# Mixer attention with the values stationary, the next layer's modulation gated by x, and the context's feed-forward moved ahead in the side work

## The chip, the cores and the metric

The kernel runs on one core of a Trainium2 chip. The time is that of one execution in device microseconds (us); a kernel's figure is the median of several runs. One run was taken with the hardware profiler, and all rows below come from that one.

## The reference, cut to what matters

A first block (gated spatial mixing, differential attention, a mixture of experts) is followed by a second block of two layers on two streams of 256 tokens by 1024 channels, `x` and `ctx`. The change touches the second block alone:

```
for layer in range(2):
    mx = split(silu(c) @ ada_w[layer] + ada_b[layer], 9)      # shifts, scales, gates of x
    mc = split(silu(c_ctx) @ ada_w[layer] + ada_b[layer], 9)  # the same of ctx
    x   = x   + 0.5*mx[2]*swiglu(modulate(rms_norm(x),   mx[0], mx[1]), gu1, down1)
    ctx = ctx + 0.5*mc[2]*swiglu(modulate(rms_norm(ctx), mc[0], mc[1]), gu1, down1)
    q, k, v, pool, fft of both streams = modulated norms @ w_in
    s = q @ k_all.T * scale;  p = softmax(s);  ax = p @ v_all   # 8 heads, 2 key/value heads
    x = x + mx[5] * concat(ax, pool mixer, fourier mixer) @ w_out
    x = x + 0.5*mx[8]*swiglu(modulate(rms_norm(x), mx[6], mx[7]), gu2, down2)
    if layer == 0: the same attention (over ctx alone), mixer and second swiglu for ctx
```

## The kernel before, in words

Everything is float32. A weight tile of 128x1024 is loaded by SP's queue into `raw`, split by ACT into `whi` (line 93) and by DVE into `wlo` (line 94), and used in three matmuls (lines 127 to 129: high by high, low by high, high by low). Activations are split alike: `hT` holds a stream's normalised channels, `T[:, 0]` those of x and `T[:, 1]` those of ctx. A helper, `norm_hT`, makes them: squares on ACT, a chain of some ten narrow DVE instructions for the inverse root (lines 146 to 157), the scaled rows `xs` (line 171, DVE), transposes on PE (line 133), then ACT and DVE write `hT`.

A feed-forward (`ffn`) is cut into 11 blocks of 256 hidden channels. A block needs four weight tiles for the gate and up halves and two for the down half. Where both streams work on a block together the matmuls are 512 columns wide and the weights are loaded once; where a stream is alone, the gate and up matmuls are 256 wide and the weights are loaded for it by itself. `CA` gives the blocks of the second feed-forward of layer 0 that ctx does alone beside x's attention (`side`), `EC` the cuts of the shared pass.

The modulation of layer 1 (`ada`, `L = 1`) is a generator of 72 steps. Each loads 128x1024 of `ada_w` into a tile `araw` and multiplies it on DVE with two vectors, summing into a column (lines 853 and 854: two instructions a step). It is advanced as weight tiles are asked for (`rate`), but its steps depend on nothing in the layer, so a gate holds them back: at step 0 the columns are first written by a copy from the tile `self.gate`, and no step can run before that copy's source has been written.

In the mixer, an attention unit is one (row half `tt`, head pair `hp`, key/value head `kv`): two score matmuls (line 1120), a maximum on DVE (1122), the exponential with its sum `s` on ACT (1124), transposes of `e` on PE (133, four for x, two for ctx), a copy to `aT` by ACT or DVE, and the product with `v` (line 1134) into the PSUM tile `po`, of which there is one. An attention of x has 16 units of 512 keys, that of ctx 16 of 256. `run(main, *rest, n)` interleaves one step of `main` with `n` of the rest. The pool mixer loads a 128x512 matrix `poolc` four times per stream into one buffer; the Fourier mixer is a short chain of matmuls.

A scheduler that estimates times writes the final order of every engine's instructions; each engine then executes its own list strictly in order.

Of the kernel before, what the change touches and what calls it, by code (L numbers as in the profile page):

```python
# [6 lines left out]
F32 = mybir.dt.float32  # L7
# [3 lines left out]
AF = mybir.ActivationFunctionType  # L11
OP = mybir.AluOpType
# [30 lines left out]
TG = ("tr",)*4  # L43
AH = 1
ME = 3
MA = 2
MP = 2
MC = 1
W1 = (4,4,4)
CA = (0, 3)  # L50
EC = (3, 6, 9, 11)
FC = (2, 6, 9, 11)
class Builder:
    def __init__(self, tc, A):
# [859 lines left out]
    def ffn(self, P, L, f, parts, cuts, pre="", ends=()):  # L914

        nc = self.nc
        gu, dn = f"gu{f}", f"dn{f}"  # L920
        nb = 7 if pre else 2 * max(b - a for a, b in zip(cuts, cuts[1:])) + 2
        for streams, c0, c1 in zip(parts, cuts, cuts[1:]):
            n = 256 * len(streams)
            act = streams[0][2] if len(streams) == 1 else self.both
            hid = []
            for j in range(c0, c1):
                if pre:
                    pp = [self.mm([128, 2, 256]) for c in range(2)]
                    pgu = [[pp[c][:, w] for c in range(2)] for w in range(2)]
                else:  # L930
                    pgu = [[self.mm([128, n], tag) for c in range(2)] for tag in ("mm", "at")]
                for w in range(2):
                    for b in range(2):
                        wt = self.W(gu, (L, 22 * w + 2 * j + b))
                        for c in range(2):
                            p = pgu[w][c] if n == 256 else pgu[w][c].rearrange("p (a b) -> p a b", a=2)
                            self.proj_T(p, [wt, wt], c, act, range(4 * b, 4 * b + 4))
                for c in range(2):
                    s = self.t(P, [128, n], F32, pre + "silu", 2)
                    fh = self.t(P, [128, n], F32R, pre + "fh", nb)  # L940
                    fl = self.t(P, [128, n], F32R, pre + "fl", nb)
                    if self.tanh:

                        nc.scalar.activation(out=s, in_=pgu[0][c], func=AF.Tanh, scale=0.5)
                        nc.vector.scalar_tensor_tensor(out=s, in0=s, scalar=1.0, in1=pgu[0][c], op0=OP.add, op1=OP.mult)
                        nc.vector.tensor_tensor(out=s, in0=s, in1=pgu[1][c], op=OP.mult)
                        nc.scalar.activation(out=fh, in_=s, func=AF.Copy, scale=0.5)
                        nc.vector.scalar_tensor_tensor(out=fl, in0=s, scalar=0.5, in1=fh.bitcast(F32), op0=OP.mult, op1=OP.subtract)
                    else:
                        nc.scalar.activation(out=s, in_=pgu[0][c], func=AF.Silu)  # L950
                        nc.vector.tensor_tensor(out=s, in0=s, in1=pgu[1][c], op=OP.mult)  # L951
                        self.split(s, fh, fl)
                    hid.append((fh, fl))
                    yield
            for c in range(2):
                out = [(x, 256 * i, g, tt) for i, (x, g, _) in enumerate(streams) for tt in range(2)]
                ps = [self.mm([128, 512], tag) for tag in ("mm", "mm", "at", "at")[: len(out)]]
                for i, j in enumerate(range(c0, c1)):
                    wh, wl = self.W(dn, (L, j, c))
                    for p, (x, off, g, tt) in zip(ps, out):  # L960
                        ts = slice(off + tt * 128, off + tt * 128 + 128)
                        for k in range(2):
                            fh, fl = hid[2 * i + k]
                            s = slice(k * 512, k * 512 + 512)
                            self.mm3(p, (fh[:, ts], fl[:, ts]), (wh[:, s], wl[:, s]), i == 0 and k == 0, j == c1 - 1 and k == 1)
                for p, (x, off, g, tt) in zip(ps, out):
                    self.gated_add(p, g, x, tt, c)
                    if c1 == cuts[-1] and c == 0 and any(x is e for e in ends):
                        self.half(x, tt)
                    yield  # L970


    def mixer(self, L, mods, d2, last, side):
# [7 lines left out]
        with tc.tile_pool(name="mix", bufs=1, reuse_waits="tile") as P:  # L981
# [127 lines left out]
            def attention(stream):  # L1109
# [1 line left out]
                d = S[nm]  # L1111
                k0, nk = (0, 4) if nm == "x" else (2, 2)
                for tt in range(2):
                    po = self.mm([128, 4, 2, 64], "ada")
                    s = self.t(P, [128, 4, 2], F32, "s", 2)
                    for hp in range(4):
                        for kv in range(2):
                            ps = self.mm([128, nk * 128], "at")
                            for i in range(2):
# [1 line left out]
                            nm_ = self.t(P, [128, 1], F32, "nm", 3)  # L1121
                            nc.vector.tensor_reduce(out=nm_, in_=ps, axis=AX.X, op=OP.max, negate=True)
                            e = self.t(P, [128, 512], F32, "e", ME)[:, : nk * 128]
                            nc.scalar.activation(out=e, in_=ps, func=AF.Exp, bias=nm_, accum_out=s[:, hp, kv : kv + 1])
                            pt = self.mm([128, nk, 128], "tr")
                            for k in range(nk):
                                self.tr(pt[:, k], e[:, k * 128 : k * 128 + 128])
# [2 lines left out]
                                nc.scalar.activation(out=aT, in_=pt, func=AF.Copy)  # L1130
                            else:
                                nc.vector.tensor_copy(aT, pt)
                            for k in range(nk):
                                nc.tensor.matmul(po[:, hp, kv], aT[:, k], v[:, k0 + k, kv * 64 : kv * 64 + 64], start=(k == 0), stop=(k == nk - 1))  # L1134
                            yield
                    nc.vector.reciprocal(s, s)
                    o = self.t(P, [128, 4, 2, 64], F32, "e", ME)
                    nc.vector.tensor_tensor(out=o, in0=po, in1=s[:, :, :, None].to_broadcast([128, 4, 2, 64]), op=OP.mult)
                    p = self.mm([128, 4, 128], "tr")
                    for hp in range(4):  # L1140
                        self.tr(p[:, hp], o[:, hp].rearrange("p k d -> p (k d)"))
                    ts = slice(tt * 128, tt * 128 + 128)
                    self.split(p, T[:, a, 0, 0:4, ts], T[:, a, 1, 0:4, ts])
                    yield

            def pool(stream):
# [47 lines left out]
            def run(main, *rest, n=1):  # L1194

                rest = chain(*rest)
                for _ in main:
                    for _ in range(n):
                        next(rest, None)
                for _ in rest:  # L1200
                    pass
# [32 lines left out]
            else:  # L1234
# [9 lines left out]
                wpf = weights(6, 4)  # L1244
                run(chain(attention(sc), kx, qx), proj(wpf, 512, sc, ev_pf), proj(wpf, 512, sx, ev_pf), pool(sc), fourier(sc), n=NA)
                run(out(sc))
                run(attention(sx), pool(sx), fourier(sx), side(), n=NF)
            run(out(sx))

    def block2(self):  # L1250
        tc, nc, A = self.tc, self.nc, self.A
        x, ctx = self.x, self.ctx
        with tc.tile_pool(name="b2", bufs=1, reuse_waits="tile") as B:
# [13 lines left out]
            def run(steps):  # L1267
                for _ in steps:
                    pass
# [21 lines left out]
            def side():  # L1291
                norm(0, 1, 6)
                cs.append(stream(0, 1, 6))
                yield
                yield from alone(0, 2, cs[0], *CA)

# [1 line left out]
            self.mixer(0, *self.mods[0], False, side)  # L1298
            self.dbg("mx0", x)
            sc, = cs  # L1300
            self.gate = T[:, 1, 1, 7].bitcast(F32)
            self.rate = RC[0]
            norm(0, 0, 6)
            sx = stream(0, 0, 6)
# [158 lines left out]
```

## Time and profile before

| | |
|---|---|
| median of 3 runs | 2257.35 us (2254.58 to 2261.62) |
| the profiled execution: time / span | 2256.36 us / 2254.6 us |
| PE (matmul) busy | 2105.7 us, 93% |
| DVE busy | 1393.9 us, 62% |
| ACT busy | 915.7 us, 41% |
| mean granted TensorE clock | 0.973 of 2.4 GHz |

PE is the engine whose list fills the span, so the reader looks for the places where PE waits and for what it waits there. The mixer of layer 0 lies at about 940 to 1192 us of the span, the second feed-forward of layer 0 from 1223 us, the mixer of layer 1 at about 1900 to 2047 us.

### The profile page before, as it was taken

How to read it: one execution, taken by the hardware profiler on the slowest of the kernel's cores; microseconds unless marked ns; L12 is line 12 of the kernel's file. 1: busy time of each engine (PE TensorE's matmuls, PEld its weight loads, DVE VectorE, ACT ScalarE, POOL GpSimd, SP SyncE). 2: the span in 40 equal slices, each digit the busy share in tenths (PEclk: the TensorE clock that was granted, in tenths of full speed). 3: DMA queues.
4: the chain of work that ended last, by engine and by line, in shares of the span. 5: the costliest groups of instructions: out<-in, count | busy, mean ns of one | idle time of the engine just before them, and what ended most of it. 6: DMA issues, size and time to landing. Idle time of an engine off the chain costs nothing.

```text
span 2254.6 us, 33045 instructions
## 1 busy us (share of the span) xinstructions
PE 2105.7 (93%) x12818; PEld 1726.8 (77%) x12818; DVE 1393.9 (62%) x2443; ACT 915.7 (41%) x1426; POOL 58.4 (3%) x109
## 2 busy tenths in 40 slices
PE   7998999889886999999994999999999999988998
PEld 5887897455464898787874888899888888877997
DVE  5778675222235555585698974368984368756665
ACT  5556553122233443465532322246322235544443
POOL 1000000000001000000000000000000000000000
PEclk9999999999998999999997999999999999998999
DMA  8645666999997777634286762246663256504553
GB/s 313 209 159 169 239 207 258 383 397 387 395 410 271 243 250 281 236 106 132 78 262 202 258 195 94 94 164 197 219 198 96 92 158 196 165 28 151 188 186 121
DMA packets 130751, 472.67 MB, mean 210 GB/s; under 512 B 15440, under 2 KB 15584, under 8 KB 130464
## 3 DMA queue, kind: packets, MB, share of 16 engines
q1 hardware_dynamic: 122976, 446.75, 56.9%
q0 software_dynamic: 7616, 23.79, 3.3%
q8 instruction: 101, 1.65, 0.3%
q14 instruction: 58, 0.48, 0.1%
HBM read 464.13 MB, written 6.34 MB: 209 GB/s over the span
## 4 chain that ended last, share of the span: by engine, by line
PE 46%; DVE 3%; issue 2%; DMA 1%; ACT 1%; DVEq 0%; ACTq 0%; POOLq 0%; POOL 0%
PE mm L127 9%; PE mm L128 9%; PE mm L129 9%; PE at L127 5%; PE at L129 5%; PE at L128 5%; PE tr L133 1%; PE ada L1134 1%; DVE wlo L94 1%; DMA araw<-ada_w 1%; DVE araw L854 1%; DVE araw L853 0%; DMA poolc<-c_pool 0%; PE at L1120 0%; DVE gadd L903 0%
## 5 line engine op out<-in xcount | busy, mean ns | idle before, releaser
L94 DVE TENSOR_TENSOR wlo<-raw,whi 128x1024 fp32r<-128x1024 f32 x440 | 538.1, 1224 | 375.0 <-ACT whi L93 369.9
L93 ACT ACTIVATE whi<-raw 128x1024 fp32r<-128x1024 f32 x440 | 466.2, 1060 | 625.0 <-PE mm L129 157.0
L128 PE MATMUL mm<-hT,whi 128*128 128x256 f32 (+1 forms) x992 | 302.6, 306 | 0.7 <-DVE hT L121 0.7
L127 PE MATMUL mm<-hT,whi 128*128 128x256 f32 (+1 forms) x992 | 301.8, 308 | 1.5 <-DVE gadd L903 1.1
L129 PE MATMUL mm<-hT,wlo 128*128 128x256 f32 (+1 forms) x992 | 301.1, 306 | 0.0
L128 PE MATMUL at<-hT,whi 128*128 128x256 f32 (+1 forms) x704 | 221.4, 315 | 0.0
L127 PE MATMUL at<-hT,whi 128*128 128x256 f32 (+1 forms) x704 | 220.8, 316 | 0.0
L129 PE MATMUL at<-hT,wlo 128*128 128x256 f32 (+1 forms) x704 | 220.5, 315 | 0.0
L127 PEld LDWEIGHTS mm<-hT,whi 128*128 128x128 f32 x992 | 186.3, 189 | 14.4 <-DVE gadd L903 1.6
L128 PEld LDWEIGHTS mm<-hT,whi 128*128 128x128 f32 x992 | 187.6, 189 | 11.2 <-DVE hT L121 1.3
L129 PEld LDWEIGHTS mm<-hT,wlo 128*128 128x128 f32 x992 | 187.1, 189 | 10.4 <-issue 0.8
L127 PE MATMUL mm<-whi,fh 128*128 128x512 f32 x440 | 173.5, 403 | 7.7 <-ACT whi L93 7.3
L128 PE MATMUL mm<-wlo,fh 128*128 128x512 f32 x440 | 175.8, 401 | 2.5 <-DVE wlo L94 2.5
L129 PE MATMUL mm<-whi,fl 128*128 128x512 f32 x440 | 173.6, 398 | 0.0
L127 PEld LDWEIGHTS at<-hT,whi 128*128 128x128 f32 x704 | 132.4, 189 | 12.5 <-ACT whi L93 1.4
L128 PEld LDWEIGHTS at<-hT,whi 128*128 128x128 f32 x704 | 132.9, 189 | 9.5
L129 PEld LDWEIGHTS at<-hT,wlo 128*128 128x128 f32 x704 | 132.6, 189 | 9.5
L94 DVE TENSOR_TENSOR wlo<-rawk,whi 128x1024 fp32r<-128x1024 f32 x72 | 88.1, 1224 | 71.7 <-ACT whi L93 69.9
L93 ACT ACTIVATE whi<-rawk 128x1024 fp32r<-128x1024 f32 x72 | 76.2, 1058 | 93.3 <-PE mm L129 37.9
L127 PEld LDWEIGHTS mm<-whi,fh 128*128 128x128 f32 x440 | 83.2, 190 | 35.7 <-ACT whi L93 12.9
L128 PEld LDWEIGHTS mm<-wlo,fh 128*128 128x128 f32 x440 | 83.7, 190 | 28.9 <-DVE wlo L94 6.3
L951 DVE TENSOR_TENSOR silu<-silu,at 128x256 f32<-128x256 f32 (+1 forms) x104 | 50.3, 486 | 82.3 <-PE at L129 81.9
(397 smaller groups left out, 4274.6 us busy)
## 6 DMA issues: line engine op xcount, KB each, us to landing
raw<-gu SPq DMA_DIRECT2D x234, 512.0 KB, 4.2
araw<-ada_w SPq DMA_DIRECT2D x144, 512.0 KB, 4.8
raw<-dn SPq DMA_DIRECT2D x118, 512.0 KB, 4.1
rawk<-w SPq DMA_DIRECT2D x65, 512.0 KB, 9.9
araw<-w SPq DMA_DIRECT2D x64, 512.0 KB, 9.9
raw<-w SPq DMA_DIRECT2D x63, 512.0 KB, 9.9
raw<-w_in SPq DMA_DIRECT2D x40, 512.0 KB, 4.3
raw<-w_out SPq DMA_DIRECT2D x28, 512.0 KB, 4.3
```

The lines of the kernel that those rows point to most:

```text
L93: self.nc.scalar.activation(out=hi[:, :cols], in_=src, func=AF.Copy)
L94: self.nc.vector.tensor_tensor(out=lo[:, :cols], in0=src, in1=hi[:, :cols].bitcast(F32), op=OP.subtract)
L127: mm(p, lh, rh, start=first, stop=False)
L128: mm(p, lh, rl, start=False, stop=False)
L129: mm(p, ll, rh, start=False, stop=last)
L133: self.nc.tensor.transpose(out, in_, self.ident[:k, :k])
L854: nc.vector.scalar_tensor_tensor(out=raw, in0=raw, scalar=1.0, in1=cb[0], op0=OP.mult, op1=OP.mult, accum_out=cols[:, 0, n : n + 1])
L951: nc.vector.tensor_tensor(out=s, in0=s, in1=pgu[1][c], op=OP.mult)
L1134: nc.tensor.matmul(po[:, hp, kv], aT[:, k], v[:, k0 + k, kv * 64 : kv * 64 + 64], start=(k == 0), stop=(k == nk - 1))
```

## The change

Four things change. The attention's product takes `v` as the stationary operand (64 columns) and the probabilities `aT` as the moving one (128 columns), once both key/value heads of a head pair have their `aT`; the result arrives channel-major, in two halves of 64 partitions, so the transposes of the output go and the softmax's division moves to `e` itself: a reciprocal and a multiplication for every unit. The gate of layer 1's modulation becomes a part of `T[:, 0]`, last written by x's norm ahead of its second feed-forward, where it was a part of `T[:, 1]`, last written by ctx's norm inside `side`. The `side` work goes ahead of pool and Fourier beside x's attention. And ctx does two blocks alone there where it did three; the third joins the shared pass.

```diff
-MA = 2
+MA = 4
...
-CA = (0, 3)
-EC = (3, 6, 9, 11)
+CA = (0, 2)
+EC = (2, 6, 9, 11)
...
-        nb = 7 if pre else 2 * max(b - a for a, b in zip(cuts, cuts[1:])) + 2
+        nb = 5 if pre else 2 * max(b - a for a, b in zip(cuts, cuts[1:])) + 2
...
                 for tt in range(2):
-                    po = self.mm([128, 4, 2, 64], "ada")
-                    s = self.t(P, [128, 4, 2], F32, "s", 2)
+                    po = self.mm([128, 4, 128], "ada")
                     for hp in range(4):
+                        aTs = []
                         for kv in range(2):
...
                             e = self.t(P, [128, 512], F32, "e", ME)[:, : nk * 128]
-                            nc.scalar.activation(out=e, in_=ps, func=AF.Exp, bias=nm_, accum_out=s[:, hp, kv : kv + 1])
+                            s = self.t(P, [128, 1], F32, "s", 4)
+                            nc.scalar.activation(out=e, in_=ps, func=AF.Exp, bias=nm_, accum_out=s)
+                            nc.vector.reciprocal(s, s)
+                            nc.vector.tensor_scalar(out=e, in0=e, scalar1=s, scalar2=None, op0=OP.mult)
                             pt = self.mm([128, nk, 128], "tr")
...
-                            for k in range(nk):
-                                nc.tensor.matmul(po[:, hp, kv], aT[:, k], v[:, k0 + k, kv * 64 : kv * 64 + 64], start=(k == 0), stop=(k == nk - 1))
+                            aTs.append(aT)
                             yield
-                    nc.vector.reciprocal(s, s)
-                    o = self.t(P, [128, 4, 2, 64], F32, "e", ME)
-                    nc.vector.tensor_tensor(out=o, in0=po, in1=s[:, :, :, None].to_broadcast([128, 4, 2, 64]), op=OP.mult)
-                    p = self.mm([128, 4, 128], "tr")
-                    for hp in range(4):
-                        self.tr(p[:, hp], o[:, hp].rearrange("p k d -> p (k d)"))
+
+                        for k in range(nk):
+                            for kv in range(2):
+                                nc.tensor.matmul(po[kv * 64 : kv * 64 + 64, hp], v[:, k0 + k, kv * 64 : kv * 64 + 64], aTs[kv][:, k], start=(k == 0), stop=(k == nk - 1))
                     ts = slice(tt * 128, tt * 128 + 128)
-                    self.split(p, T[:, a, 0, 0:4, ts], T[:, a, 1, 0:4, ts])
+                    self.split(po, T[:, a, 0, 0:4, ts], T[:, a, 1, 0:4, ts])
...
-                run(attention(sx), pool(sx), fourier(sx), side(), n=NF)
+                run(attention(sx), side(), pool(sx), fourier(sx), n=NF)
...
-            self.gate = T[:, 1, 1, 7].bitcast(F32)
+            self.gate = T[:, 0, 1, 7].bitcast(F32)
```

The first place is x's norm ahead of the second feed-forward of layer 0, on DVE (`gadd` and `x` are the last sums of the mixer's output, `rsv`, `rsy` and `rsh` the chain of the inverse root, `araw` a modulation step). Before:

```order
L903 TENSOR_TENSOR gadd<-mm,grow 128x512
L146 TENSOR_SCALAR rsv_11434<-ss,ssp 128x1
L854 SCALAR_TENSOR_TENSOR araw,acols<-araw 128x1024
L904 TENSOR_TENSOR x<-x,gadd 128x512
L147 TENSOR_SCALAR rsy_11435<-rsv_11434 128x1
L853 SCALAR_TENSOR_TENSOR araw,acols<-araw 128x1024
L151 TENSOR_SCALAR rsh_11436<-rsy_11435,rsv_11434 128x1
L146 TENSOR_SCALAR rsv_11449<-ss,ssp 128x1
L854 SCALAR_TENSOR_TENSOR araw,acols<-araw 128x1024
```

Now, at the same place:

```order
L903 TENSOR_TENSOR gadd<-mm,grow 128x512
L146 TENSOR_SCALAR rsv_11322<-ss,ssp 128x1
L904 TENSOR_TENSOR x<-x,gadd 128x512
L147 TENSOR_SCALAR rsy_11323<-rsv_11322 128x1
L151 TENSOR_SCALAR rsh_11324<-rsy_11323,rsv_11322 128x1
L157 SCALAR_TENSOR_TENSOR rsy_11323<-rsh_11324,rsy_11323 128x1
```

Seven modulation instructions stood between the last `gadd` and the first `xs` of this norm; none does now. All 144 of them follow the norm.

The second place is PE at the end of ctx's output projection in layer 0 (the three matmuls with `whi` and `wlo` are its last; `qT` are x's queries, `e` its exponentials, `poolc` the pool matrix). Before:

```order
L127 MATMUL mm<-whi,hT 128x512
L128 MATMUL mm<-wlo,hT 128x512
L129 MATMUL mm<-whi,hT 128x512
L1120 MATMUL at<-araw,qT 128x512 x2
L1154 MATMUL mm<-poolc,pf 64x256 x2
L1120 MATMUL at<-araw,qT 128x512 x2
L133 MATMUL tr<-ident,e 128x128 x4
```

Now:

```order
L129 MATMUL mm<-whi,hT 128x512
L1120 MATMUL at<-araw,qT 128x512 x10
L133 MATMUL tr<-ident,e 128x128 x4
L1120 MATMUL at<-araw,qT 128x512 x2
L1141 MATMUL ada<-aT,v 64x128
L133 MATMUL tr<-ident,xs 128x128 x12
L127 MATMUL mm<-hT,whi 128x256 x2
```

The transposes of ctx's norm (`xs`) now follow twelve score matmuls, where the whole of x's attention with its pool and Fourier steps stood ahead of them.

The third place is PE in x's attention, some 250 rows later in layer 0, behind ctx's down projection (`lfl`). Now:

```order
L129 MATMUL mm<-whi,lfl 128x512
L1141 MATMUL ada<-aT,v 64x128 x8
L133 MATMUL tr<-ident,e 128x128 x4
L1154 MATMUL mm<-poolc,pf 64x256 x2
L133 MATMUL tr<-ident,e 128x128 x4
L1120 MATMUL at<-araw,qT 128x512 x4
L1141 MATMUL ada<-aT,v 64x128 x8
L1154 MATMUL mm<-poolc,pf 64x256 x2
L1120 MATMUL at<-araw,qT 128x512 x4
```

Here before stood x's output projection; the last six units' scores of x's attention and all pool and Fourier steps of x moved behind ctx's feed-forward.

## Rows read from the trace of the kernel before

**Rows 1.** Who waited for whom, PE, 900 to 1260 us: total, times, longest.

```profile
PE tr L133 <- DVE xs L171: 27.0, 2, 24.9
```

**Rows 2.** PE in time, end of layer 0's mixer: start, us, instruction, [idle].

```profile
1165.96 0.47 PE L127 MATMUL mm<-whi,hT 128*128 128x512 f32 x1 [1.82 <-DVE gadd L903]
...
1191.35 0.39 PE L129 MATMUL mm<-whi,hT 128*128 128x512 f32 x1
...
1222.92 0.78 PE L127 MATMUL mm<-hT,whi 128*128 128x256 f32 x2
```

**Rows 3.** PE in order of time, end of layer 1's mixer.

```profile
2046.03 0.39 PE L128 MATMUL mm<-wlo,hT 128*128 128x512 f32 x1
2046.26 0.40 PE L129 MATMUL mm<-whi,hT 128*128 128x512 f32 x1
2052.95 1.08 PE L133 MATMUL tr<-ident,xs 128*128 128x128 f32 x4 [6.29 <-DVE xs L171]
...
2057.56 0.78 PE L127 MATMUL mm<-hT,whi 128*128 128x256 f32 x2
```

**Rows 4.** DVE in order of time, x's norm after layer 0's mixer.

```profile
1203.81 0.69 DVE L903 TENSOR_TENSOR gadd<-mm,grow 128x512 f32<-128x512 f32 x1
...
1204.53 1.22 DVE L854 SCALAR_TENSOR_TENSOR araw<-araw 128x1024 f32<-128x1024 f32 x1
...
1215.83 0.75 DVE L171 TENSOR_SCALAR xs<-x,rsy 128x1024 f32<-128x1024 f32 x1
```

**Rows 5.** Windows, all engines: us, busy of PE, PEld, DVE, ACT, POOL; clock, DMA.

```profile
1220.00:1230.00 10.00, 8.86 (x53) 8.42 (x54) 6.24 (x14) 3.85 (x7) 1.03 (x2) 0.65 0.17 53
1250.00:1300.00 50.00, 48.87 (x249) 40.76 (x248) 48.46 (x75) 16.55 (x21) 0.00 (x0) 1.00 0.78 262
2057.00:2067.00 10.00, 10.00 (x76) 10.00 (x76) 5.81 (x8) 6.15 (x10) 0.00 (x0) 0.86 0.03 5
```

**Rows 6.** PE in order of time, layer 1's attention, steady stretch and end.

```profile
1997.09 0.60 PE L133 MATMUL tr<-ident,e 128*128 128x128 f32 x4
...
1997.99 1.89 PE L1134 MATMUL ada<-v,aT 128*128 128x64 f32 x16
...
2000.63 0.60 PE L133 MATMUL tr<-ident,e 128*128 128x128 f32 x4
...
2026.45 0.66 PE L133 MATMUL tr<-ident,e 128*128 128x128 f32 x4 [0.78 <-DVE e L1138]
2027.80 0.50 PE L127 MATMUL mm<-whi,hT 128*128 128x512 f32 x1 [0.69 <-ACT hT L120]
```

**Rows 7.** DVE in order of time, layer 1's attention.

```profile
1997.35 0.69 DVE L1122 TENSOR_REDUCE nm<-at 128x1 f32<-128x512 f32 x1 [1.73 <-PE at L1120]
1997.96 0.68 DVE L1132 COPY aT<-tr 128x512 f32<-128x512 f32 x1
...
2002.70 0.19 DVE L1136 RECIPROCAL s<-s 128x8 f32<-128x8 f32 x1
```

**Rows 8.** One line: durations ns min/median/max, first and last start.

```profile
L171 DVE TENSOR_SCALAR xs<-x,rsy x4: 746/752/754, 953.8 to 1219.1; 128x1024 f32<-128x1024 f32 x4
```

**Rows 9.** PE in order of time, float32 matmuls of several widths.

```profile
81.25 1.92 PE L882 MATMUL ada<-araw,cc 128*32 128x512 f32 x14
...
1069.39 0.66 PE L133 MATMUL tr<-ident,e 128*128 128x128 f32 x4 [2.60 <-ACT e L1124]
...
1078.04 1.08 PE L1154 MATMUL mm<-poolc,pf 128*64 128x256 f32 x4
1079.05 2.00 PE L1134 MATMUL ada<-v,aT 128*128 128x64 f32 x16
...
1083.18 1.08 PE L1154 MATMUL mm<-poolc,pf 128*64 128x256 f32 x4 [0.32 <-DMA poolc<-c_pool]
...
1087.36 1.03 PE L1173 MATMUL mm<-fftc,pf 128*128 128x256 f32 x4
1088.22 0.60 PE L133 MATMUL tr<-ident,e 128*128 128x128 f32 x4
```

## The prediction

> **What bounds the kernel now.** The page's busy times come first: PE 93%, DVE 62%, ACT 41%. PE's list fills the span, so only its waits and its own instructions count. The waits of PE by cause come second. Around the mixer of layer 0 one line stands far above all others: PE's transposes waited 27.0 us, 24.9 of them at once, for `xs`, the scaled rows that DVE makes in x's norm [rows 1]. PE in order of time shows the place: the last matmul of x's output projection starts at 1191.35, the first of the next feed-forward at 1222.92, 31.57 us later [rows 2]. The same code at the end of layer 1's mixer takes 11.30 us, from 2046.26 to 2057.56, of which the wait for `xs` is 6.29 [rows 3]. DVE in order of time says why the two differ: between the last `gadd` at 1203.81 and the first `xs` at 1215.83 lie twelve microseconds, filled with modulation steps of the next layer at 1.22 us an instruction, in a chain whose own links are 128x1 [rows 4]. DVE was late before that already: PE waited 1.82 us for a `gadd` ahead of x's output projection, and this projection ran from 1165.96 to 1191.58 (last start plus one step), 25.6 us, though its 96 matmuls at the 0.233 us between two starts in layer 1 make 22.4 [rows 2, 3].
>
> In the attention itself PE is dense. In layer 1 two units (one head pair) take 3.54 us, from 1997.09 to 2000.63, with no wait between [rows 6].
>
> **The change part by part.**
>
> *The gate.* The order shows all modulation steps behind x's norm. What goes: 31.57 less 11.30, 20.3 us; the loss inside and ahead of the output projection, 25.6 less 22.4 plus 1.82, 5.0 us; and some of the slow clock. The granted clock was 0.65 in the ten microseconds from 1220, so about 7 of them ran at the lower of the two levels, 4 of these with matmuls; in layer 1 it was 0.86 in the ten from 2057, some 2.2 us of matmuls at the lower level [rows 5]. Half of the difference is 1 us. Together 26 us; at least the 20.
>
> The modulation's 144 instructions, at most 1.22 us each, do not vanish. They now run beside the second feed-forward. There the trace has the same mixture: from 1250 to 1300 DVE was busy 48.5 of 50 us and PE 48.9 [rows 5], so the cover costs at most 1.1 us in 50, in blocks where x is alone, of which there is one less. I book nothing. But the steps now reach the norms of layer 1's first feed-forward: the order has one step's instruction inside x's norm chain and about a dozen in ctx's. The cover is a feed-forward of two blocks of the other stream, 192 narrow matmuls, half of 0.233 us each, 22 us, and the down half. A dozen steps of 1.22 us are 15. I take +2; without the cover, +8.
>
> *The third block in the shared pass.* PE streams as many columns as before; six weight tiles fewer are split by ACT and DVE, neither of which sets the end there. Nothing. So do the buffer counts, which only let both `aT` of a pair wait for the joint product.
>
> *The product with v.* Sixteen passes per head pair of x stay, now with 128 moving columns instead of 64. A float32 pass of 256 columns takes 0.215 us (four from 1087.36 to 1088.22), so 128 take 0.107 and 16 in series 1.72, which is what the 16 passes of before, 1.89 with their end, take too [rows 6, 9]. They write alternate halves of the partitions. That such passes run side by side the modulation of layer 0 shows: 14 passes of 512 columns into quarters took 1.92 us, where 14 times 0.43 would be 6.0 [rows 9]. Two halves then give 0.86. Against it: entering and leaving the half-width form. Four half-width passes took 1.01 us to the next start, 0.15 more than four full ones [rows 9]; the entry's share doesn't show, I take 0.2 in all. The order cuts a pair's product in two pieces, so 0.4 a pair, and a gain of 0.46. The Trainium skill, TensorEngine Tiling (Array Packing), section Key Properties, speaks against the swap here: changing the tiling mode drains the engine. The trace agrees with 0.15 us and no more; if the drain also kept the halves apart, the sum would be that of the rival below.
>
> DVE gets a reciprocal and a multiplication for each unit. The reciprocal took at most 0.19 us; the multiplication is bounded by half of `xs` of 1024 columns, 0.75/2, and by the 0.68 of a 512-column pass; I take 0.40, since `xs` is the same form [rows 7, 8]. A pair then costs DVE two maxima and a copy at 0.61 each and 1.1 of new work, 2.9 us. That is below 3.54, but not far below what PE would need. I take −0.25 us for each of the 16 pairs of x, −4. Bounds: −0.64 a pair (DVE's 2.9), −10; +0.4 a pair on all 24 with no overlap, +10. In ctx's attention, with half the keys, overlap and changes cancel, and the longer chain of each unit costs some waits: +1.5.
>
> *The output's transposes.* At the end of layer 1's attention PE waited 0.78 us for the division and 0.69 for the split behind the transposes, and the clock fell afterwards [rows 6]. Now the split reads `po` directly. −2. The same at the other ends lies beside other work.
>
> *Side work first.* Ctx's norm in layer 0 loses its cover. Before, its transposes came behind nearly all of x's attention; now twelve score matmuls, four transposes and a little stand between them and ctx's output projection (the second place). The uncovered norm is 11.3 us as in layer 1 [rows 3]; here six units' maxima, multiplications and exponentials stand between its links on DVE and ACT, six times 0.61 and more, so 15. PE's own work in it is 3.5 us (12 times 0.233, 0.4 of transposes, one product). Of the 11.5 left, before already lost 2.60 us waiting for the first exponential at the same place, and about 1 to the clock [rows 9]. +8; bounds +4 and +12.
>
> At the other end, the third place, the pool matrices must follow one another through one buffer. From the end of one use, 1079.05, to the next one's start with its transfer just waited for, 1083.18, are 4.1 us [rows 9]. Between two uses PE now has 2.4 to 3.1 us of work by the order, three times. That is 3 to 5 us, and the Fourier chain at the end has little left beside it: +4; bounds 0 and +8. Before, other work covered all but 0.32.
>
> Sum: −26 −4 +1.5 −2 +8 +4 +2 = −16.5 on the profiled execution's 2256.4, which is 1.0 below the median: 2240 for such an execution, 2241 for the median.
>
> **The rivals.** *The swap pays and the norm is covered better* (2222 to 2235): halves run side by side with no change to pay, DVE's 2.9 us become the pair's time (−10), and ctx's norm costs 4. The 14 passes speak for it; that DVE's list is strictly in order, with a reciprocal waiting for ACT in front of the next maximum, speaks against it.
>
> *What the gate gives is eaten* (2251 to 2264, no change): the swap has no overlap (+10 for −4), ctx's norm costs 12 and the pool chain 8; −16.5 becomes +5.5 with all three and +1.5 with the first and one other. For it: every wait that is added stands on PE's own list. Against it: two or three separate sizes have to come out badly.
>
> *The modulation stalls another norm* (above 2264, slower): the steps that left x's norm in layer 0 stand in front of ctx's norm in layer 1, and the shared pass waits for it. Price: the excess of layer 0, 20 us, and the lost projection time again; with −16.5 and +2 replaced by +26 it ends at 2265. It decides from the point where ctx's norm takes more than its cover, the two blocks of x, some 33 us. For it: about a dozen of these steps in its chain, each waiting for a load. Against it: cover of 33 us for a chain of 11 plus 15.
>
> *The gate does nothing*: excluded by the order, which has no modulation instruction ahead of x's norm.
>
> **How the numbers follow.** Forecast (2235 to 2251) 0.55; larger gain 0.20, with 0.03 more below 2222; eaten 0.15; slower 0.07. The time is that of the forecast, 2241. The range of 8 in 10 reaches into both neighbours, 2226 to 2257; the forecast's own is 2235 to 2251. A measurement of this kernel tells about 0.3%, 6.8 us, from no change: faster than 2250.6 has 0.78, within 0.15, slower 0.07.
>
> **What would show it.** Right: the line of PE's waits for `xs` at the end of layer 0's mixer falls from 24.9 us to 6 or 7; from the last matmul of x's output projection to the first of the feed-forward are 11 to 12 us; a new wait for ctx's `xs` of 5 to 10 us appears behind ctx's projection; a head pair in layer 1 takes 3.2 to 3.4 us; `poolc` transfers appear among PE's waits with some microseconds. Wrong: a pair at or above 3.54 us (no overlap); no wait at ctx's norm; a wait of PE for `xs` in layer 1's first feed-forward beyond 10 us; or DVE's lists so full beside the second feed-forward that PE waits for `wlo` there.

## The result, and the profile after

The changed kernel takes 2275.08 us (median of 10 runs, 2267.92 to 2279.58), the kernel before 2259.23 (10 runs, 2254.58 to 2263.61); the ratio is 1.0066, with a 95% interval of 1.0050 to 1.0083. It is slower by some 16 us, where 16 us of gain were forecast, and lies outside the range, 2226 to 2257.

| profiled execution | before | after |
|---|---|---|
| span, us | 2254.6 | 2270.9 |
| PE busy, us | 2105.7 | 2116.0 |
| DVE busy, us | 1393.9 | 1401.3 |
| matmuls | 12818 | 12698 |
| mean granted clock | 0.973 | 0.974 |

PE has 120 instructions less and is "busy" 10 us longer. The mean of one matmul `mm<-hT,whi` (L127) rose from 308 to 312 ns in the page's groups, but most of that is the mix: 224 of 960 are 512 columns wide, where 208 of 992 were. With the forms kept apart it is 286 ns after 284 at 256 columns and 400 after 397 at 512. So single matmuls do take a little longer, the first sign of a loss which the waits show only in part.

What the gate was meant to do is there. The waits of PE around layer 0's mixer, 900 to 1260 us (the counterpart of [rows 1]), from the view of who waited for whom (total, times, longest):

```profile
PE tr L133 <- DVE xs L171: 8.2, 3, 6.2
PE at L1120 <- ACT e L1125: 6.5, 5, 2.9
PE tr L133 <- ACT hft L223: 2.7, 3, 0.9
PE at L129 <- DVE wlo L94: 2.2, 1, 2.2
PE mm L1154 <- DMA poolc<-c_pool: 2.0, 2, 1.6
```

And PE in order of time at the end of that mixer (the counterpart of [rows 2]):

```profile
1152.44 0.58 PE L127 MATMUL mm<-whi,hT 128*128 128x512 f32 x1
...
1174.81 0.39 PE L129 MATMUL mm<-whi,hT 128*128 128x512 f32 x1
1181.35 0.90 PE L133 MATMUL tr<-ident,xs 128*128 128x128 f32 x3 [6.15 <-DVE xs L171]
...
1185.78 0.78 PE L127 MATMUL mm<-hT,whi 128*128 128x256 f32 x2
```

The output projection takes 22.6 us (25.6 before), and from its last matmul to the first of the feed-forward are 10.97 us (31.57 before).

Where the time went is seen when the span is cut at instructions that both kernels have. The marks are PE's first transposes of x's norm ahead of layer 0's mixer (936.64 before, 937.05 after), the first matmul of x's output projection (1165.96, 1152.44), the first of the feed-forward behind it (1222.92, 1185.78), the first transposes of x's norm ahead of layer 1's mixer (1871.14, 1887.92), the first matmul of layer 1's second feed-forward (2057.56, 2072.32), and the end. The third block of ctx moved from the second stretch into the fourth; it has 96 matmuls at 0.1173 us from start to start and 24 at 0.2344, as the feed-forward shows them, 16.9 us, for which the table corrects. Differences to before, in us, of one profiled execution each (the experiments e1 to e12 follow below):

| kernel | to mark 1 | mixer 0 | projection and norm of x | feed-forwards | mixer 1 | rest | span |
|---|---|---|---|---|---|---|---|
| after | +0.4 | +3.0 | -23.6 | **+37.0** | -2.0 | +1.5 | +16.3 |
| e1, gate alone | -1.0 | -2.8 | -23.8 | **+34.2** | 0.0 | +1.4 | +7.9 |
| e2, all but the gate | +0.3 | +7.8 | -3.0 | +6.9 | -2.8 | +1.5 | +10.8 |
| e3, after + own row | 0.0 | +2.6 | -23.7 | +25.2 | -2.5 | +1.4 | +3.1 |
| e4, after + ctx gate for the third group | -1.2 | +5.9 | -23.7 | +24.8 | -2.0 | +0.7 | +4.5 |
| e5, both | +4.5 | +5.2 | -23.6 | +5.3 | -3.8 | +1.9 | -10.5 |
| e6, before + gate + both | -0.5 | -6.2 | -23.8 | **-0.9** | +0.3 | +1.3 | -29.7 |
| e7, product alone | +0.6 | -2.4 | +2.9 | +2.4 | -1.5 | +1.8 | +3.9 |
| e8, order alone | +1.4 | +5.9 | -3.7 | +4.9 | +0.2 | -0.1 | +8.7 |
| e9, cut alone | +1.5 | +4.2 | +0.1 | +7.7 | +0.4 | -0.2 | +13.6 |
| e10, e6 + product + cut | +2.9 | -1.1 | -23.8 | +7.0 | -2.1 | -0.3 | -17.4 |
| e11, e6 + product | +6.4 | -6.9 | -23.8 | +0.1 | -3.2 | +1.4 | -26.0 |
| e12, e6 + order | +4.0 | +5.6 | -23.6 | +0.9 | +0.8 | +2.2 | -10.1 |

The first column is code that no edit touches; it differs by up to 7.4 us between executions, so single entries of a few microseconds prove little. The row of e5 comes from an execution of 2245.90 us, 8.8 above the median of that kernel. The row of the changed kernel is plain: 23.6 us gained at x's norm, 37.0 lost between the last passes of layer 0's second feed-forward and the first of layer 1's.

The windows of that stretch, for the kernel after (length; busy us of PE, PEld, DVE, ACT, POOL; granted clock; DMA share; GB/s):

```profile
1440.00:1460.00 20.00, 20.00 (x93) 16.41 (x92) 19.73 (x33) 2.12 (x2) 0.00 (x0) 1.00 0.64 211
1460.00:1480.00 20.00, 17.50 (x125) 15.91 (x124) 20.00 (x29) 8.19 (x9) 0.00 (x0) 1.00 0.74 250
1480.00:1500.00 20.00, 17.31 (x100) 16.03 (x99) 19.35 (x33) 7.62 (x11) 0.00 (x0) 0.83 0.72 230
1500.00:1520.00 20.00, 16.59 (x101) 14.03 (x100) 18.48 (x32) 4.92 (x9) 0.00 (x0) 0.91 0.78 256
1520.00:1540.00 20.00, 18.51 (x142) 17.37 (x141) 19.52 (x44) 12.80 (x21) 1.55 (x3) 1.00 0.72 226
1540.00:1560.00 20.00, 18.26 (x115) 15.55 (x114) 16.03 (x23) 10.77 (x17) 0.54 (x1) 1.00 0.56 193
1560.00:1580.00 20.00, 19.21 (x144) 17.98 (x143) 19.12 (x41) 11.87 (x20) 0.00 (x0) 1.00 0.72 242
1580.00:1600.00 20.00, 12.21 (x44) 7.91 (x42) 19.04 (x35) 4.05 (x5) 0.00 (x0) 0.87 0.64 222
1600.00:1620.00 20.00, 19.50 (x76) 15.68 (x77) 19.47 (x32) 5.61 (x8) 0.00 (x0) 0.87 0.54 177
sum 180.00, PE 159.10 PEld 136.87 DVE 170.73 ACT 67.93 POOL 2.09; mean PE 17.68 PEld 15.21 DVE 18.97 ACT 7.55 POOL 0.23
```

The same view and windows of the kernel before, two of the nine and the sum:

```profile
1480.00:1500.00 20.00, 20.00 (x173) 20.00 (x172) 12.28 (x15) 9.77 (x14) 0.00 (x0) 1.00 0.49 160
...
1580.00:1600.00 20.00, 20.00 (x89) 16.10 (x88) 18.74 (x30) 7.48 (x9) 0.00 (x0) 1.00 0.60 200
...
sum 180.00, PE 179.60 PEld 157.30 DVE 133.92 ACT 79.32 POOL 2.08; mean PE 19.96 PEld 17.48 DVE 14.88 ACT 8.81 POOL 0.23
```

After, PE stood idle for 180 - 159.1 = 20.9 us of these 180, and ran four windows partly at the lower of its two clock levels: (0.17 + 0.09 + 0.13 + 0.13) of 20 us are up to 10.4 us of work not done (up to, since some of the slow time can fall into idle time). Together they are some 31 us; before it was 0.4. The rest of the 37.0 is about what the cut costs in kernels that do not have this loss (5.3 to 7.7, in e2, e5, e9 and e10). DVE is the engine that is full instead: 170.7 of 180 us, 133.9 before. No single wait tells this: PE's waits in this stretch have twelve causes, none above 5.6 us in all and 3.2 at once. At x's norm in layer 0, before the change, one wait of 24.9 us stood out.

### The profile page after: what moved, and what is told of

Its sections match the earlier page's. It is cut to its first block, busy times and chain, and to the rows that moved or that the text cites. A ratio compares the mean times of both kernels' runs of the same rounds, so it can differ in the third digit from the quotient of the medians.

```text
span 2270.9 us, 32814 instructions
## 1 busy us (share of the span) xinstructions
PE 2116.0 (93%) x12698; PEld 1711.2 (75%) x12698; DVE 1401.3 (62%) x2517; ACT 912.5 (40%) x1418; POOL 57.8 (3%) x109
## 5 line engine op out<-in xcount | busy, mean ns | idle before, releaser
L94 DVE TENSOR_TENSOR wlo<-raw,whi 128x1024 fp32r<-128x1024 f32 x434 | 530.0, 1222 | 391.7 <-ACT whi L93 383.4
L93 ACT ACTIVATE whi<-raw 128x1024 fp32r<-128x1024 f32 x434 | 459.4, 1060 | 639.0 <-PE mm L129 167.8
L127 PE MATMUL mm<-hT,whi 128*128 128x256 f32 (+1 forms) x960 | 295.6, 312 | 4.6 <-DVE gadd L903 3.3
L128 PE MATMUL mm<-hT,whi 128*128 128x256 f32 (+1 forms) x960 | 296.9, 311 | 1.8 <-DVE hT L121 1.8
L129 PE MATMUL mm<-hT,wlo 128*128 128x256 f32 (+1 forms) x960 | 295.2, 310 | 2.9 <-DVE wlo L94 2.9
L127 PE MATMUL at<-hT,whi 128*128 128x256 f32 (+1 forms) x704 | 223.8, 322 | 4.4 <-DVE gadd L903 3.6
L128 PE MATMUL at<-hT,whi 128*128 128x256 f32 (+1 forms) x704 | 225.0, 320 | 0.0
L127 PEld LDWEIGHTS mm<-hT,whi 128*128 128x128 f32 x960 | 181.2, 191 | 19.1 <-DVE gadd L903 4.5
L129 PEld LDWEIGHTS mm<-hT,wlo 128*128 128x128 f32 x960 | 182.1, 191 | 14.8 <-DVE wlo L94 3.5
L128 PEld LDWEIGHTS mm<-hT,whi 128*128 128x128 f32 x960 | 182.6, 190 | 13.8 <-DVE hT L121 3.0
L127 PE MATMUL mm<-whi,fh 128*128 128x512 f32 x440 | 173.3, 402 | 10.4 <-ACT whi L93 7.3
L127 PEld LDWEIGHTS at<-hT,whi 128*128 128x128 f32 x704 | 133.8, 192 | 17.9 <-DVE gadd L903 4.0
L128 PEld LDWEIGHTS at<-hT,whi 128*128 128x128 f32 x704 | 134.7, 191 | 10.4
L94 DVE TENSOR_TENSOR wlo<-rawk,whi 128x1024 fp32r<-128x1024 f32 x72 | 88.1, 1223 | 76.1 <-ACT whi L93 75.7
L127 PEld LDWEIGHTS mm<-whi,fh 128*128 128x128 f32 x440 | 83.2, 190 | 38.9 <-ACT whi L93 12.9
L129 PEld LDWEIGHTS mm<-whi,fl 128*128 128x128 f32 x440 | 84.1, 192 | 24.0 <-DVE fl L121 4.6
```

Of the source, the lines that this page charges most:

```text
L93: self.nc.scalar.activation(out=hi[:, :cols], in_=src, func=AF.Copy)
L94: self.nc.vector.tensor_tensor(out=lo[:, :cols], in0=src, in1=hi[:, :cols].bitcast(F32), op=OP.subtract)
L127: mm(p, lh, rh, start=first, stop=False)
L128: mm(p, lh, rl, start=False, stop=False)
L129: mm(p, ll, rh, start=False, stop=last)
```

## The experiments

Theory A: DVE's list carries the modulation, 72 steps in three groups of 24. The gate moved the groups to places where DVE has no room. Theory B: the loss comes from the attention, the order or the cut.

The trace after shows two links for A. In order of time, all engines (`acols<-acols,abias` at L859 closes a group's sums; L870 copies the group's transposed results to `r`, L872 sends them out; L853 is a step; L841 is the gate of the second and the third group: the copy is made anew at steps 24 and 48, not at step 0 alone; the last `ctx` sum and `xs<-ctx` frame ctx's norm in layer 1):

```profile
1298.79 0.20 DVE L859 TENSOR_TENSOR acols<-acols,abias 128x48 f32<-128x48 f32 x1
...
1417.34 0.38 PE L133 MATMUL ada<-ident,acols 128*8 128x128 f32 x2
...
1418.74 0.36 ACT L870 ACTIVATE araw<-ada 8x256 f32<-8x256 f32 x1
...
1419.39 1.03 POOL L872 DMA_DIRECT2D ada<-araw  x2 [240.41 <-ACT araw L870]
...
1419.54 1.22 DVE L853 SCALAR_TENSOR_TENSOR araw<-araw 128x1024 f32<-128x1024 f32 x1
...
1530.34 0.19 DVE L859 TENSOR_TENSOR acols<-acols,abias 128x48 f32<-128x48 f32 x1
...
1554.64 0.68 DVE L904 TENSOR_TENSOR ctx<-ctx,gadd 128x512 f32<-128x512 f32 x1
...
1560.86 0.19 DVE L841 COPY acols<-hT 128x48 f32<-128x48 f32 x1
...
1588.20 0.74 DVE L171 TENSOR_SCALAR xs<-ctx,rsy 128x1024 f32<-128x1024 f32 x1
```

The kernel before, the same view:

```profile
1222.62 0.21 DVE L859 TENSOR_TENSOR acols<-acols,abias 128x48 f32<-128x48 f32 x1
...
1227.65 0.38 PE L133 MATMUL ada<-ident,acols 128*8 128x128 f32 x2
...
1335.12 0.21 DVE L859 TENSOR_TENSOR acols<-acols,abias 128x48 f32<-128x48 f32 x1
...
1555.33 0.68 DVE L904 TENSOR_TENSOR ctx<-ctx,gadd 128x512 f32<-128x512 f32 x1
...
1562.59 0.75 DVE L171 TENSOR_SCALAR xs<-ctx,rsy 128x1024 f32<-128x1024 f32 x1
...
1585.50 0.18 DVE L841 COPY acols<-hT 128x48 f32<-128x48 f32 x1
```

Link one: before, PE's two transposes of the first group ran at 1227.65, 5 us after DVE had it and 11 us behind the end of the long wait for x's norm, and the second group was done by 1335. After, DVE has the first group at 1298.79, but the transposes stand at 1417.34 in PE's list, 119 us later. ACT's copy and POOL, which sends the results out, follow them (of POOL's 240 us of idle time the first half lies ahead of 1298.79). The second group's steps begin 2 us behind the transposes and end at 1530, beside the narrow passes at the end of the feed-forward. Link two: the third group's gate opened behind ctx's norm at 1585.50 before, and opens ahead of it at 1560.86 after. From ctx's last sum to its first `xs` are 33.6 us (1554.64 to 1588.20), where they were 7.3 (1555.33 to 1562.59). In these 33.6 us DVE's list has eleven instructions of modulation steps, 14.3 us with their short accumulator reads, and nine splits of weight tiles (L94), 11.0 us, where the 7.3 us before held no step and three splits, 3.7 us.

**e1, the gate alone** on the kernel before:

```diff
-            self.gate = T[:, 1, 1, 7].bitcast(F32)
+            self.gate = T[:, 0, 1, 7].bitcast(F32)
```

> The kernel before with one edit: self.gate is x's hT in place of ctx's. Theory A (the modulation's second and third groups of 24 steps now run where passes of 256 columns, which leave DVE little room, and the norms of layer 1 stand): PE's wait for xs at the end of layer 0's mixer falls from 24.9 to 6 to 8 us, about 34 us are lost later between the last pass of layer 0's FFN2 and the first pass of layer 1's FFN1, and the time is 2272 us (2264 to 2280). Theory B (the loss comes from the attention, the order beside it or the cut of the FFN, and the gate only gains): 2238 us (2232 to 2243), with nothing lost in that stretch.

Measured: 2263.53 us against 2257.27, ratio 1.0021 (1.0006 to 1.0036). Not B: the loss of 34.2 us is there with the gate alone. The total missed A's range by half a microsecond, since the gate gains 27 us (23.8 and 2.8 ahead of it), where I had counted only the wait, 18.7.

**e2, the changed kernel with ctx's gate**, the reverse of the edit above.

> The changed kernel with the gate put back to ctx's hT, all else kept. Theory A: the 34 us lost around the end of layer 0's FFN2 are back, the wait for xs behind layer 0's out-projection returns to some 20 to 25 us; 2275 - 34 + 18 = 2259 us (2250 to 2266). Theory B: only the wait returns, 2275 + 18 = 2293 us (2286 to 2300).

Measured: 2264.82 us, 1.0037 (1.0022 to 1.0052). The feed-forward stretch is at +6.9 in place of +37.0, B's 2293 is out; but the rest of the change costs 7.5 us by itself, +7.8 in mixer 0 and +6.9 in the feed-forward, with 5.8 back in the projection and in mixer 1.

**e3, `r` in a buffer of its own** on the changed kernel. `r` was one of five buffers that the steps take turns in, so a step waits until `r` is copied out:

```diff
-                r = self.t(G, [8, 2, 128], F32, "araw", 5)
+                r = self.t(self.B if L else G, [8, 2, 128], F32, "arow" if L else "araw", 1 if L else 5)
...
-MA = 4
+MA = 3
```

> The changed kernel, where the small tile that takes a group's 24 results to DRAM (r) has a buffer of its own instead of one of the five that the modulation's steps take turns in (MA goes from 4 to 3 to make room). Theory A with the buffer as the link (the second group waits from 1299 to 1420 us for the transposes of the first, which stand at 1417 us in PE's queue): the second group runs from about 1300 us, beside 512-column passes, the 19 us lost between 1460 and 1560 us mostly go, the 15 us between 1560 and 1620 us stay; 2256 us (2250 to 2264). Theory B, or A with another link: 2275 us (2271 to 2279).

Measured: 2261.53 us, 1.0023 (1.0007 to 1.0039). That is 4.3 us above the kernel before, where the whole change was 15.9 above it, so some 12 us came back. DVE and PE in order of time, then the windows 1300 to 1400 of e3 and of the kernel after:

```profile
1300.99 0.20 DVE L859 TENSOR_TENSOR acols<-acols,abias 128x48 f32<-128x48 f32 x1
...
1350.77 0.38 PE L133 MATMUL ada<-ident,acols 128*8 128x128 f32 x2
...
1398.61 0.20 DVE L859 TENSOR_TENSOR acols<-acols,abias 128x48 f32<-128x48 f32 x1
```

```profile
1300.00:1400.00 100.00, 100.00 (x431) 80.35 (x430) 91.85 (x144) 25.15 (x29) 1.03 (x2) 1.00 0.70 220
...
1300.00:1400.00 100.00, 100.00 (x429) 80.41 (x428) 38.05 (x42) 24.13 (x28) 0.00 (x0) 1.00 0.28 95
```

The second group begins at 1302.56 and is done at 1398.61, though the first one's transposes come only at 1350.77: it no longer waits for them, and beside the shared passes it costs PE nothing (DVE busy 91.9 of 100 us, 38.1 in the kernel after; PE 100 and clock 1.00 in both). So the buffer was the link. What the third group costs stayed, 25.2 us in the feed-forwards with the cut's share.

**e4, the third group gated by ctx again**, on the changed kernel:

```diff
             ffn(0, 2, [(sx,), (sx, sc), (sx, sc), (sx,)], (0, *EC), (x,))
 
+            self.gate = T[:, 1, 1, 7].bitcast(F32)
             self.need(1, 1)
```

> The changed kernel, where the gate is set back to ctx's hT behind layer 0's FFN2, so that only the third group of modulation steps waits for ctx's norm of layer 1 as it did before. Theory A: the steps no longer stand in front of that norm, PE does not stall there, 15 us or most of them come back: 2260 us (2255 to 2268). Theory B: 2275 us (2271 to 2279).

Measured: 2260.06 us, 1.0013 (1.0001 to 1.0026). DVE in order of time shows ctx's norm with no step in it again, 9.4 us from last sum to `xs`:

```profile
1558.91 0.69 DVE L904 TENSOR_TENSOR ctx<-ctx,gadd 128x512 f32<-128x512 f32 x1
...
1568.34 0.75 DVE L171 TENSOR_SCALAR xs<-ctx,rsy 128x1024 f32<-128x1024 f32 x1
...
1591.29 0.18 DVE L841 COPY acols<-hT 128x48 f32<-128x48 f32 x1
```

**e5, both edits** on the changed kernel.

> The changed kernel with both edits of e3 and e4 (r in a buffer of its own, the gate back to ctx's hT behind layer 0's FFN2). The two losses lie in stretches that follow each other (1460 to 1560 and 1560 to 1620 us). If they are independent, both go and the gains of e3 (some 11 us) and e4 (some 12 us) add: 2248 us (2242 to 2253), faster than the kernel before. If they are one backlog of VectorE that either edit works off, the second brings nothing: 2258 to 2262 us.

Measured: 2237.14 us against 2257.40, 0.9916 (0.9891 to 0.9941). The time lies 5 us below the range for two independent losses: against the kernel before, the two edits together bring 36 us, e3 alone 11.6 and e4 alone 13.1. (Two of the six runs took 2245.90 and 2251.06, the others 2233.90 to 2237.54.) So the two losses are not independent: in the windows 1440 to 1620 the one that is left costs 22.6 us in e3 and 17.1 in e4, counted as above, more together than the 31 of both; why was not tried. The stretch's 37.0 us became 5.3. The windows 1440 to 1620 sum up as before:

```profile
sum 180.00, PE 179.60 PEld 157.39 DVE 136.34 ACT 77.96 POOL 2.09; mean PE 19.96 PEld 17.49 DVE 15.15 ACT 8.66 POOL 0.23
```

**e6, the gate and both edits on the kernel before** (`nb`, the number of buffers for the hidden tiles of a stream that works alone, 6 to make room), attention, order and cut untouched.

> The kernel before with x's hT as gate and the same two edits (nb goes from 7 to 6 to make room for r), attention, order and cut as before. The gate alone took some 27 us from the mixer's end and lost 32 us later; with the loss gone 2236 us (2230 to 2243). If the loss has another source than the two groups of steps: 2258 to 2265 us, as the gate alone.

Measured: 2228.64 us against 2257.40, 0.9872 (0.9856 to 0.9889): 29 us faster than the kernel before and the fastest of all here. The gate's gain is kept (-6.2 and -23.8), the loss is -0.9. The count `nb` changed with it; in e5, where the stretch's loss went as well, it did not.

**e7, the product alone** (the whole edit of the attention, `MA` 3, `nb` 6), and **e11, the product on e6** (`MA` 2).

> The kernel before with the attention's new product alone (values stationary, division on e, no output transposes; MA 3, nb 6), gate, order and cut as before. The prediction's terms: -4 -2 +1.5, that is 2253 us (2249 to 2256). Rival (the division in each unit's chain lets PE wait for e): 2260 us or more.

> The kernel of e6 with the attention's new product alone in addition (MA 2, since r's buffer leaves no more room). The prediction's terms -4 -2 +1.5: 2224 us (2220 to 2226). What it cost alone in e7, +3.5: 2232 us (2229 to 2235); e10's 2237.6 us then leaves +6 for the cut.

Measured: e7 2260.90 us, 1.0020 (1.0009 to 1.0031); e11 2230.50 us against 2258.10, 0.9878 (0.9856 to 0.9900), which is 1.9 above e6. Both missed the figure of the prediction's terms and fell into the range of the other: the rival's in e7, the "what it cost alone" in e11. The rival's mechanism isn't what the traces show: from 930 to 1180 us PE waits 4.6 us for `e` from ACT in e7 where it waited 3.8 before. In the two mixers the product does what the terms said: -2.4 and -1.5 in e7, and against e6 -0.7 and -3.5 in e11. Yet neither kernel is faster for it. In e7 5.3 us more go at x's norm and in the feed-forward; in e11 the profiled execution lost 6.9 us more than e6 ahead of every edit. Over the whole kernel the product gains nothing in these runs; alone it costs 2 to 7 us by the interval.

**e8, the order alone**, and **e12, the order on e6**:

```diff
-                run(attention(sx), pool(sx), fourier(sx), side(), n=NF)
+                run(attention(sx), side(), pool(sx), fourier(sx), n=NF)
```

> The kernel before with the order alone changed (context's norm and FFN2 blocks ahead of pool and Fourier beside x's attention), all else as before. The prediction's terms: 8 us for the uncovered norm and 4 us for the tail, 2269 us (2262 to 2275). Rival (the attention covers the norm, or what the norm loses the tail gives back): 2257 us (2254 to 2260).

> The kernel of e6 with the order alone in addition (context's part ahead of pool and Fourier). The prediction's terms +8 and +4: 2240 us (2235 to 2244). What it cost alone in e8, +7.3: 2236 us (2232 to 2239). If the order only hurt through the modulation's steps beside it: 2229 us (2226 to 2231).

Measured: e8 2264.73 us, 1.0029 (1.0013 to 1.0046); e12 2245.72 us, 0.9945 (0.9923 to 0.9967), 17 above e6. e8 lies in the range of the prediction's terms; e12 lies above all three of its figures. In the mixer the order costs 5.6 + 6.2 = 11.8 us in e12, near the 12 of the prediction; in e8 half of that. There the modulation's steps still run in the mixer; what they do to the difference was not tried. The profiled executions of e12 and e6 are 19.6 apart; the other 7.8 are spread over the other stretches, 4.5 of them ahead of every edit.

**e9, the cut alone** (`CA` (0, 2), `EC` (2, 6, 9, 11), `nb` 5), and **e10, product and cut on e6**.

> The kernel before with the cut of layer 0's FFN2 alone (CA (0, 2), EC (2, 6, 9, 11), nb 5). The prediction gave it no term, since the block that leaves ctx's part goes into a pass that takes x and ctx together: 2257 us (2254 to 2260). If the parts add up, the change without its gate (e2, +7.5 us) less e7 (+3.5) and e8 (+7.3) leaves -3: 2254 us.

> The kernel of e6 with the attention's new product and the cut in addition (MA 3, nb 5): only the order of the context's part is left as before. If the product brings its few microseconds once the modulation is out of the way (the prediction's -4 -2 +1.5): 2224 us (2220 to 2227). If it costs what it cost alone (+3.5) and the cut brings 3: 2229 us (2226 to 2233).

Measured: e9 2271.15 us against 2257.02, 1.0061 (1.0040 to 1.0081); e10 2237.60 us, 0.9912 (0.9886 to 0.9939). Both expectations failed for e9, and both for e10: the cut costs 14 us alone and about 7 on e11. In the kernels with the cut and without the gate's loss (e2, e5, e9, e10) the feed-forward stretch holds 5.3 to 7.7 us more; in the uncut ones it is -0.9 to 2.4, but 4.9 in e8. The place is the start of the second feed-forward: in its first 80 us (from 1183 in e10, from 1198 in e11) PE is idle for 4.0 us and loses 6.4 to the clock in e10, 1.6 and 1.2 in e11. The count `nb` goes with the cut, 5 for 7 in e9 and 5 for 6 in e10, so the cut and the smaller count are not told apart. The parts do not add up (3.5 + 7.3 + 14 for e2's 7.5): order and cut, each bad alone, cost no more together than the cut (by their medians e5 and e10 are level). Why the shared pass after two narrow blocks loses 7 us, with DVE at 18.7 of 20 us from 1245 to 1265 in e9, was not tried.

## Why the prediction was wrong

*The gate, -26:* right. Mixer 0 and x's projection with norm give -26.6 in e1 and -30.0 in e6.

*The modulation's new place, "I book nothing" and "I take +2; without the cover, +8":* this is the step that failed. It is 31 us in the windows after, and 31.7 of the 37.0 come back with the two edits. Three things were wrong in it. I gave a price to the steps that stand inside the norms of layer 1 alone, a dozen instructions, and none to the groups: the second group, done at 1335 us before, now ran from 1419 to 1530. I read the cover from a window [rows 5] with PE at 48.9 of 50 us and took it for one in which x is alone; but matmuls of 256 columns run there only until 1260, then a down half and from 1276 on a shared pass, all 512 wide. At the end of the feed-forward the passes are of one stream, and a weight tile, 1.22 us on DVE, is used up in 2.8 us (24 matmuls at 0.1173) instead of 5.6. A step is 2.4 us more. And the clock fell, which took up to a third of the loss.

*The rival "the modulation stalls another norm":* it had the right place and sign for half of it, and its threshold was met: ctx's norm takes 33.6 us where "some 33" were named. I gave it 0.07, for "cover of 33 us for a chain of 11 plus 15". The chain alone takes 7.3 us (before) or 9.4 (e4), less than the 11, and the steps' 14.3 us are near the 15; what the sum left out are the nine splits of weight tiles for x's passes, 11.0 us, which stand in the same list of DVE. The passes of x that were to cover the norm draw on the very list that was full. The other half, the second group held by `r`, was in no rival. It hangs on something I had in hand: PE's transposes of the first group follow other rows in PE's list after than before. That the wait of 24.9 us, behind which they ran before, had been the gap that let them in fits the rows of all kernels with the new gate, but was not tried by itself.

*The cut, 0:* wrong, by 5 to 8 us in the feed-forward and, in e9 and e10, some 4 to 6 in the mixer. It rested on DVE and ACT, "neither of which sets the end there"; yet in the 80 us from the feed-forward's start in e10 PE waits 1.4 us for `wlo` and 1.1 for `fl`, both of DVE.

*The product, -4, with the transposes, -2, and ctx's attention, +1.5:* the sum is near what the mixers gave (-3.9 in e7), but not by the way that was forecast, so the nearness is luck. The pair was named as the test, "a pair at or above 3.54 us (no overlap)". It took 3.54 us again, so nothing was gained in the steady stretch. PE in order of time, layer 1 after (the counterpart of [rows 6]):

```profile
2017.72 1.09 PE L1141 MATMUL ada<-aT,v 128*64 128x128 f32 x14
2018.74 0.66 PE L133 MATMUL tr<-ident,e 128*128 128x128 f32 x4
2019.15 0.71 PE L1120 MATMUL at<-araw,qT 128*128 128x512 f32 x2
2019.79 0.43 PE L1141 MATMUL ada<-aT,v 128*64 128x128 f32 x2
2020.16 0.73 PE L1120 MATMUL at<-araw,qT 128*128 128x512 f32 x2
2020.73 0.60 PE L133 MATMUL tr<-ident,e 128*128 128x128 f32 x4
2021.26 1.09 PE L1141 MATMUL ada<-aT,v 128*64 128x128 f32 x14
```

From start to start, the product takes 1.02 + 0.37 = 1.39 us where the 16 passes took 1.72. The 14 passes take 0.65 us more than the 2, twelve passes at 0.054, half of the 0.107 to 0.109 that one takes by itself, so the halves do run side by side. But the four groups beside the product take 0.41 + 0.64 + 0.57 + 0.53 = 2.15 us, where 3.54 - 1.72 = 1.82 were left for them. The 0.33 gained is lost again.

The same view, asked for stretches of some 0.02 to 0.1 us, shows single passes of this pair:

```profile
2017.72 0.33 PE L1141 MATMUL ada<-aT,v 128*64 128x128 f32 x2
...
2018.43 0.38 PE L1141 MATMUL ada<-aT,v 128*64 128x128 f32 x2
...
2018.54 0.27 PE L1141 MATMUL ada<-aT,v 128*64 128x128 f32 x1
...
2019.95 0.27 PE L1141 MATMUL ada<-aT,v 128*64 128x128 f32 x1
```

Two passes start together at 2017.72, but the last two of the 14 start one behind the other, at 2018.43 and 2018.54, and so do the two that stand apart, at 2019.79 and 2019.95. Four of the 16 run alone: the list puts two of them behind the next scores, away from the two that they could run beside. In pairs the four would take two times 0.109 us, alone they take four, 0.22 us more. That an unbroken product would keep its gain was not tried. The four changes of width cost the rest: by the single starts 0.14 to 0.20 us each, 0.63 in all, where I had 0.4. The 0.22 and the 0.23 above my 0.4 make up the 0.46 that I had booked as gain. The gain in layer 1 is at its end: no transposes of the output, and 0.69 us for the split alone in front of the projection.

*The order, +8 and +4:* the size is near, 11.8 in e12's mixer. The wait for ctx's `xs` that was forecast, 5 to 10 us, is 1.5 in the kernel after. In e12 PE is busy 33.4 us from 1060 to 1100 where it is 37.8 in e6, and the clock (0.87 and 0.62 in two of the four windows of 10 us, 1.00 in e6) takes up to 5.1 more. The kernel after has its clock at 0.50 from 1070 to 1080. Its waits for `e` (6.5 us in five) are not all of the order, since 4.6 of them stand in e7 too. `poolc` cost 2.0, where 4 were booked. Beside product and cut, e5 against e10, the order costs 6.3 in the mixer of the profiled executions and nothing in the medians.

Of the signs of failure one came true beside the pair: "DVE's lists so full beside the second feed-forward that PE waits for `wlo` there". From 1440 to 1556 DVE is busy 109.6 of 116 us after the change, and PE waits 3.2 us for `wlo` and 7.3 for `gadd`, another of DVE's tiles. The sign was named, and no term of the sum had a price for it. "A wait of PE for `xs` in layer 1's first feed-forward beyond 10 us" never came; the loss is spread over twelve causes and the clock, and its whole size is seen in windows only.

## What to carry to other kernels

Work that hides on a second engine has a place as well as a price. Ask of an edit that delays it not only which instructions now stand in a chain, but where each whole group ends up, what width of pass runs there, and which shared buffer lets the next group start. Here two small edits to buffer and gate turned 6 us of loss into 29 us of gain, and the edits that came along with the gate were worth nothing or less.

A removed wait may also have been the gap in which other instructions found their place: see where they go.

## What the runs showed of the hardware

Float32 passes into the two halves run side by side, twelve of them in 0.65 us; two passes without partners start 0.11 and 0.16 us apart. A change between full-width and half-width passes costs 0.14 to 0.20 us here, an estimate from the single starts above: 16 passes side by side would take 16 x 0.107 / 2 = 0.86 us and took 1.39, the groups beside them 0.33 more, together 0.86, of which 0.22 are the passes that run alone and some 0.63 four changes. The Trainium skill, TensorEngine Tiling (Array Packing), section Key Properties, says that changing the tiling mode drains the engine; the trace agrees as far as each change costs time, and puts a size on it.

A full DVE costs PE twice: in the windows after, 20.9 us were idle and up to 10.4 more went to the lower clock level, granted 0.83 to 0.91 in four of the nine windows.
